# Layer 0's head by halves of the tokens, with another order of its first loads, in a two-layer float32 trunk on one core

## Chip, core and metric

One NeuronCore of a Trainium2 chip runs the kernel. The metric is the time of one execution in device microseconds. The engines are TensorE (PE; PEld is its weight load), VectorE (DVE), ScalarE (ACT), GpSimd (POOL) and SyncE (SP, which here issues most DMAs); 16 DMA engines move the data.

## The reference, cut to what matters

The model is one inference step of two layers over 640 tokens of width 1024: 128 prompt tokens, which take one condition vector, and 512 sample tokens, which take another.

```python
for i in range(2):
    sh, sc, gt = split(silu(cond) @ ada_w[i] + ada_b[i])   # adaLN, for both conditions
    h = rms_norm(y, norm_g[i]) * (1 + sc) + sh
    # layer 0: a, gate, z = split(h @ w_in + b_in); v = a * sigmoid(gate)
    #          v = depthwise_conv(v, 31 taps); v = silu(layer_norm(v))
    #          out = (v * silu(z)) @ w_out
    # layer 1: bidirectional state-space branch, chunked scan, gated norm, @ w_out
    y = y + gt * out
return rms_norm(y, final_norm_g)                           # and layer 1's final states
```

All is float32. A product with float32 accuracy is made of three matmuls in a reduced 32-bit format: each operand is split into a high part and the remainder, and high x high, high x low and low x high are added up in PSUM.

## The kernel before, in words

Channels lie on the 128 partitions: x is eight tiles (index k) of 128 channels by 640 tokens. The tokens are kept as two halves of 320, each with 64 prompt tokens ahead of 256 sample tokens. A tile product of layer 0 multiplies 128 output channels' weights with all eight k: per k and half three matmuls of 320 columns, so 48 in all. There are 48 tiles: a0 to a15, gates g0 to g15 (tile numbers 16 to 31) and z0 to z15.

The head of layer 0 is what the change is about; it runs in a scope of its own, with its own tiles. `loads` issues on SP first the constants, then x, k by k, and then for each of the eight adaLN blocks two pieces of 512 KB of w_ada (tile wa), with the weights of the first three tiles (u16, u0, u17; tile wf, 512 KB each) behind blocks 0, 1 and 2. `square0` squares x on ACT, `sums0` adds up the squares over the channels on PE into the tile rps, takes the root and the reciprocal for 640 tokens and spreads the result to all partitions (rs0). `ada_chain(k)` makes block k's scale and shift: eight small matmuls for each piece of w_ada into the tile ada, a copy of the row on ACT, a turn on PE (the matmul with ada_row), a bias on DVE (mod) and a scale on ACT (gsc). `modulation0(k)` then makes `modo = x * gsc * rs0` on DVE, h_hi (rounded, with the shift) on ACT and h_lo (the remainder) on DVE, each in one instruction for the prompt tokens of both halves and one for the sample tokens of both. `first_split` splits the weights of the first three tiles (high part wh on ACT, remainder wl on DVE or POOL), and `firsts` multiplies: for each k the three tiles u16 (in the trace u__99), u0 (u__100) and u17 (u__297), six matmuls each.

Behind the head `filler` runs the other 45 products in the order of PLAN0. A gate tile's sigmoid and its a tile give v; the depthwise convolution of tile i adds 31 taps on v: one is the start on ACT (cva), `NPOOL[i]` of them are made on ACT and added on POOL, the others are DVE instructions (line 808). The sums for the layer norm are made on PE behind products, as tiles become ready, the last two of them by `late_sums` (tile pst); `stats` spreads mean and inverse deviation (tile pmr), and then come normalising, gating and the output products.

The order on each engine is fixed when the program is built. Each step is a chain of operations with an assumed duration; a planner (`Order`) takes at each turn the operation that could begin first, by its model of the engines, and breaks ties by the table PRIO0. On the chip each engine works in that order and waits at an instruction whose inputs aren't there. DMAs from SP are issued in order, with at most eight on their way: the ninth waits for the landing of the first.

## Time and profile before

| | |
|---|---|
| Median of 3 runs (lowest to highest) | 1072.1 us (1069.98 to 1072.92) |
| Profiled execution, its own time | 1072.78 us |
| Its span, first to last instruction | 1071.0 us |
| Mean granted TensorE clock | 0.993 |
| PE busy / PEld | 1043.6 us (97%) / 973.2 us |
| DVE / ACT / POOL busy | 798.2 / 655.2 / 456.3 us |
| HBM read | 140.73 MB, 136 GB/s over the span |

Span times count from the first instruction; the execution's own time is 1.8 us longer. Busy shares are means over stages with different limits: PE's 97% says that it rarely stands still, not where. Where it does is read from windows and from the timeline, rows of which stand below.

### The profile page before, as it was taken

To read this page: it belongs to the slowest core of one execution; us is meant where nothing else is said; L and a number is where in the kernel's file an instruction comes from. 1 tells how busy PE (TensorE), PEld (TensorE's weight loads), DVE (VectorE), ACT (ScalarE), POOL (GpSimd) and SP (SyncE) were. 2 spreads that over 40 slices of the span, in tenths; PEclk is the share of its full clock that TensorE was granted. 3 is DMA by queue.
4 is the path that set the end of the run, shared out by engine and by line. 5 is a ranking of instruction groups with operands and counts; after the bars stand their busy time and mean duration, and the time that the engine had idled before them with its cause. 6 is when DMAs were issued, how large, how long until landed. Compare 5 with 4: busy or idle time off the path is not lost.

```text
span 1071.0 us, 19887 instructions
## 1 busy us (share of the span) xinstructions
PE 1043.6 (97%) x7892; PEld 973.2 (91%) x7892; DVE 798.2 (75%) x1191; ACT 655.2 (61%) x1081; POOL 456.3 (43%) x459
## 2 busy tenths in 40 slices
PE   5999999999999999999999999999999999999996
PEld 3899999999999999999999988998889988988886
DVE  2589999998997689103788787889767766985763
ACT  5468788787686588333576666685438553663542
POOL 0029989978596401110000155405532373445313
PEclk9999999999999999999999999999999999999998
DMA  9488888788766667675122644332633234343102
GB/s 358 193 248 205 195 218 197 177 212 209 175 142 135 144 133 157 151 170 114 59 75 73 142 102 128 93 95 71 147 83 96 89 99 129 108 101 107 41 21 99
DMA packets 86413, 146.94 MB, mean 137 GB/s; under 512 B 26800, under 2 KB 49712, under 8 KB 86320
## 3 DMA queue, kind: packets, MB, share of 16 engines
q1 hardware_dynamic: 77680, 114.73, 35.8%
...
q14 instruction: 31, 0.25, 0.1%
HBM read 140.73 MB, written 4.92 MB: 136 GB/s over the span
## 4 chain that ended last, share of the span: by engine, by line
PE 85%; DVE 7%; ACT 4%; DMA 2%; issue 1%; SPq 0%; POOL 0%; DVEq 0%; ACTq 0%
PE pz L1281 8%; PE o L1281 8%; PE xs L1281 4%; PE po L1563 3%; PE o L1819 3%; PE pst L1500 2%; DVE xs L1325 2%; PE C L1281 2%; PE B L1281 2%; PE py L1631 2%; PE o__4958 L156 1%; PE o__5267 L156 1%; PE o__5258 L156 1%; PE o__5245 L156 1%; PE o__5238 L156 1%; PE o__4948 L156 1%
## 5 line engine op out<-in xcount | busy, mean ns | idle before, releaser
L808 DVE SCALAR_TENSOR_TENSOR cva<-v,cst,cva 128x550 f32<-128x550 f32 (+12 forms) x346 | 270.1, 822 | 11.7 <-ACT cva L800 6.6
L880 POOL TENSOR_TENSOR cv<-cv,tp 128x490 f32<-128x490 f32 (+5 forms) x134 | 172.9, 1290 | 8.5
L839 ACT ACTIVATE tp<-v,cst 128x490 f32<-128x490 f32 (+5 forms) x134 | 92.4, 718 | 36.8 <-POOL cv L880 36.3
L423 ACT CAST wh<-wf 128x1024 fp32r<-128x1024 f32 x63 | 65.9, 1046 | 63.6 <-PE o__5267 L156 30.1
L1243 ACT CAST wh<-wf 128x1024 fp32r<-128x1024 f32 x53 | 55.5, 1046 | 66.5 <-PE pz L1281 24.4
L1281 PE MATMUL o<-yhl,wh 128*128 128x320 f32 x384 | 93.0, 329 | 0.0
L1281 PE MATMUL pz<-h_hi,wh 128*128 128x320 f32 x256 | 86.9, 339 | 0.0
L1569 POOL TENSOR_TENSOR y<-y,yo 128x512 f32<-128x512 f32 x32 | 47.2, 1474 | 75.9 <-DVE yo L1567 75.7
L1281 PE MATMUL pz<-h_hi,wl 128*128 128x320 f32 x256 | 79.1, 309 | 0.0
L1281 PE MATMUL pz<-h_lo,wh 128*128 128x320 f32 x256 | 79.0, 309 | 0.0
L1247 DVE TENSOR_TENSOR wl<-wf,wh 128x1024 fp32r<-128x1024 f32 x47 | 63.8, 1358 | 17.6 <-ACT wh L1243 17.5
L1281 PE MATMUL xs<-h_hi,wh 128*128 128x320 f32 x224 | 74.3, 332 | 0.8 <-ACT up L1312 0.8
L1281 PEld LDWEIGHTS o<-yhl,wh 128*128 128x128 f32 x384 | 64.0, 188 | 7.8 <-issue 7.8
L1281 PE MATMUL xs<-h_hi,wl 128*128 128x320 f32 x224 | 69.3, 309 | 0.1
L1281 PE MATMUL xs<-h_lo,wh 128*128 128x320 f32 x224 | 69.2, 309 | 0.0
L1325 DVE SCALAR_TENSOR_TENSOR xs<-up,cst,xs 128x642 f32<-128x642 f32 x64 | 62.6, 981 | 4.6 <-PE rms L1685 2.1
L433 ACT ACTIVATE wl<-wh 128x1024 fp32r<-128x1024 f32 x58 | 61.5, 1061 | 1.7
L1444 ACT ACTIVATE gf<-gf,cols 128x128 f32<-128x128 f32 x160 | 50.2, 390 | 18.0 <-DVE gf L1440 17.8
L434 POOL DMA_DIRECT2D wl<-w_in x43 | 37.5, 873 | 54.7 <-ACT wl L433 51.7
L1281 PE MATMUL o<-yhl,wl 128*128 128x320 f32 x192 | 59.4, 309 | 0.0
L1438 POOL TENSOR_TENSOR gb<-gb,cols 128x512 f32<-128x512 f32 x20 | 24.0, 1198 | 79.2 <-DVE xs L1325 65.1
L1281 PEld LDWEIGHTS pz<-h_hi,wh 128*128 128x128 f32 x256 | 48.3, 189 | 4.2 <-issue 4.2
...
## 6 DMA issues: line engine op xcount, KB each, us to landing
...
```

The source lines that it names most:

```text
L156: T.matmul(ps[:, b, at : at + t1 - t0], lhsT=w, rhs=h[:, t0:t1], start=first and n == 0, stop=last and n == 2)
L423: t = yield op(ACT, 1.05, lambda: S.copy(out=wh, in_=wf))
L433: yield op(ACT, 1.06, lambda: S.activation(out=wl, in_=wh.bitcast(F32), func=AF.Copy, scale=-1.0))
L808: t = yield op(VE, 0.24 + 0.01 * (hi - lo), lambda: V.scalar_tensor_tensor(out=rows64(accs[i], lo, hi), in0=rows64(vs[i], lo + d, hi + d), ...
L839: t = yield op(ACT, 0.72, lambda: S.activation(out=tp[:, :, 0 : hi - lo], in_=rows64(vs[i], lo + d, hi + d), func=AF.Copy, scale=w_dw(i, t ...
L880: t = yield op(PO, 1.3 + 0.019 * (hi - lo - 49), lambda: G.tensor_add(out=rows64(cv[i], lo, hi), in0=rows64(cv[i], lo, hi), in1=sgs["tp", ...
L1243: S.copy(out=cell["wh"], in_=cell["wf"])
L1247: e_.tensor_sub(out=cell["wl"], in0=cell["wf"], in1=cell["wh"].bitcast(F32))
L1281: T.matmul(ps[:, b, at_ : at_ + t1 - t0], lhsT=w_, rhs=t_[:, t0:t1], start=k == 0 and n == 0, stop=k == nk - 1 and n == 2)
L1325: t = yield op(VL, 0.89, lambda: V.scalar_tensor_tensor(out=acc, in0=u[:, d : d + PW], scalar=c("w_c", j * 5 + d), in1=acc, op0=ALU.mult, ...
L1444: t = yield op(ACT, 0.39, lambda: S.activation(out=gv[:, h_, :], in_=gv[:, h_, :], func=AF.Exp, bias=cols1[ch][:, o8 + h_ : o8 + h_ + 1]), ...
L1569: t = yield op(PO, 1.29, lambda: G.tensor_add(out=y, in0=y, in1=yo))
```

## The change

x is loaded as two halves of the tokens, each in four DMAs of two k; the squares of a half go to ACT or DVE, whichever the planner finds earlier; the sums, the root and the spread are made for each half apart, in a tile of the ring that held the adaLN rows. The third first tile, u17, gets its PSUM tile from the start (in the new program it is u__101). `modulation0` and `firsts` run for each half as chains of their own: half the columns in each instruction, twice as many instructions; the matmuls keep their 320 columns and their number, 144. The order of the first loads is now a list, LOADS0: x, block 0, the weights of u16 and u0, block 1, the weights of u17, then blocks 2 to 7. The tables PRIO0, PLAN0 and NPOOL have new values. One buffer of the ring st goes (11 to 10), and rs0 gets a tile of its own.

```diff
--- before.py
+++ after.py
@@ -38,11 +38,12 @@
 
 
...
-PLAN0 = "a1 z0 g2 a2 g3 a3 g4 a4 g5 a5 g6 a6 g7 a7 g8 a8 g9 a9 g10 z1 z2 a10 z3 g11 a11 g12 a12 g13 a13 g14 z4 a14 g15 z5 z6 a15 z7 z8 z9 z10 z11 z12 z13 z14 z15"
-NPOOL = (12, 6, 12, 6, 12, 11, 8, 10, 2, 8, 9, 8, 12, 4, 6, 8)
...
+PLAN0 = "a1 g2 a2 g3 a3 g4 a4 z0 g5 a5 g6 a6 g7 a7 g8 a8 g9 a9 g10 a10 g11 a11 g12 z1 z2 z3 a12 g13 a13 g14 a14 g15 a15 z4 z5 z6 z7 z8 z9 z10 z11 z12 z13 z14 z15"
+NPOOL = (9, 10, 12, 10, 3, 7, 11, 6, 12, 10, 12, 3, 9, 11, 3, 2)
+LOADS0 = (("x", 0), ("x", 1), ("a", 0), ("w", 0), ("w", 1), ("a", 1), ("w", 2), ("a", 2), ("a", 3), ("a", 4), ("a", 5), ("a", 6), ("a", 7))
 
 
@@ -437,7 +438,10 @@
 
 
         def stt(name):
-            return sp.tile([P, NT], F32, tag="st", bufs=11, name=name)
+            return sp.tile([P, NT], F32, tag="st", bufs=10, name=name)
+
+        def stt0(name):
+            return sp.tile([P, NT], F32, name=name)
 
         wa0, w0, x_sq, psx = {}, {}, {}, []
 
@@ -445,9 +449,12 @@
             def load(kb, fn, name):
                 t = yield op(DM, kb / 345.0, fn)
                 post(name, t + 2.2)
-            for k in range(KD):
-                yield from load(328, lambda: nc.sync.dma_start(out=x[k], in_=a["x"][:, k, :]), ("x", k))
-            for k in range(KD):
+            def load_x(b):
+                tok = slice(b * HN, b * HN + HN)
+                for k in range(0, KD, 2):
+                    yield from load(328, lambda: nc.sync.dma_start(out=xs_[:, k : k + 2, tok], in_=a["x"][:, k : k + 2, tok]), ("x", k, b))
+
+            def load_ada(k):
                 for q in range(2):
                     yield get("wa")
 
@@ -455,20 +462,24 @@
                         w = wa0[k, q] = sp.tile([P, 1024], F32, tag="wa", bufs=12, name="wa")
                         nc.sync.dma_start(out=w, in_=a["w_ada"][k, :, q * 1024 : q * 1024 + 1024])
                     yield from load(524, load_a, ("wa0", k, q))
-                if k < 3:
-                    if k < 2:
-                        yield get("wf")
-                        pool, bufs = gp, (2, 3, 3)
-                    else:
-                        pool, bufs = sp, (1, 1, 1)
-
-                    def load_w():
-                        w0["f", k] = pool.tile([P, 1024], F32, tag="wf", bufs=bufs[0], name="wf")
-                        nc.sync.dma_start(out=w0["f", k], in_=a["w_in1"][(16, 0, 17)[k]])
-                    yield from load(524, load_w, ("wf", k))
-                    start(first_split(k, pool, bufs), 0.0)
                 start(ada_chain(k), 0.0)
-                start(modulation0(k), 0.0)
+                for b in range(2):
+                    start(modulation0(k, b), 0.0)
+
+            def load_first(n):
+                if n < 2:
+                    yield get("wf")
+                    pool, bufs = gp, (2, 3, 3)
+                else:
+                    pool, bufs = sp, (1, 1, 1)
+
+                def load_w():
+                    w0["f", n] = pool.tile([P, 1024], F32, tag="wf", bufs=bufs[0], name="wf")
+                    nc.sync.dma_start(out=w0["f", n], in_=a["w_in1"][(16, 0, 17)[n]])
+                yield from load(524, load_w, ("wf", n))
+                start(first_split(n, pool, bufs), 0.0)
+            for what, n in LOADS0:
+                yield from {"x": load_x, "a": load_ada, "w": load_first}[what](n)
             yield from load(303, lambda: nc.sync.dma_start(out=cst0[0], in_=a["cst"][:, NCST : NCST + NCST0]), ("cst0",))
             run.clock[SP] = run.clock[DM] - 1.0
             start(weights(), run.clock[DM] - 1.0)
@@ -492,36 +503,40 @@
                 put("wf", t)
             post(("w0", n), t)
 
-        def square0():
-            yield get("px")
-            psx.append(px.tile([P, 2, 512], F32, tag="x", bufs=1, name="rps"))
-            rps = psx[0]
+        def square0(b):
+            yield get("adp")
+            ps = sps.tile([P, 512], F32, tag="ada", bufs=2, name="rps")
             for k in range(KD):
-                yield key(("x", k))
+                yield key(("x", k - k % 2, b))
                 yield get("st")
-
-                def square():
-                    x_sq[k] = stt("rms_sq")
-                    S.activation(out=x_sq[k], in_=x[k], func=AF.Square)
-                t = yield op(ACT, 0.73, square)
-                start(sums0(k, rps), t)
-
-        def sums0(k, rps):
-            t = yield op(PE, 0.4, lambda: quarter_sums(rps[:, 0, 320:480], x_sq[k], k == 0, k == KD - 1))
+                sq = stt("rms_sq")[:, 0:HN]
+                xv = x[k][:, b * HN : b * HN + HN]
+                t = yield either((ACT, 0.42, lambda: S.activation(out=sq, in_=xv, func=AF.Square)), (VL, 0.44, lambda: V.tensor_mul(out=sq, in0=xv, in1=xv)), bias=0.1)
+                start(sums0(k, b, ps, sq), t)
+
+        def sums0(k, b, ps, sq):
+            def add_up():
+                for q in range(2):
+                    r = 64 * b + 32 * q
+                    T.matmul(ps[r : r + 32, 0:QN], lhsT=ones[:, 0:32], rhs=sq[:, q * QN : q * QN + QN], start=k == 0, stop=k == KD - 1)
+            t = yield op(PE, 0.2, add_up)
             put("st", t)
             if k < KD - 1:
                 return
-            rq = sp.tile([P, QN], F32, name="rq0")
-            yield op(ACT, 0.42, lambda: S.activation(out=rq, in_=rps[:, 0, 320:480], func=AF.Sqrt, scale=1.0 / 1024, bias=epsb))
+            rows = slice(64 * b, 64 * b + 64)
+            rq = sp.tile([P, QN], F32, name=f"rq0{b}")[rows]
+            yield op(ACT, 0.42, lambda: S.activation(out=rq, in_=ps[rows, 0:QN], func=AF.Sqrt, scale=1.0 / 1024, bias=epsb[rows]))
             yield op(VE, 1.2, lambda: V.reciprocal(out=rq, in_=rq))
-            t = yield op(PE, 1.2, lambda: quarter_spread(rps, rq))
-            rs0.append(stt("rs0"))
-            t = yield op(ACT, 0.72, lambda: S.copy(out=halves(rs0[0]), in_=rps[:, :, 0:HN]))
-            put("px", t)
-            post(("rs0",), t)
-            yield op(ACT, 0.25, lambda: S.activation(out=junk, in_=rs0[0][:, 0:1], func=AF.Sigmoid), "sig")
-
-        rs0 = []
+
+            def spread_rq():
+                for q in range(2):
+                    T.matmul(ps[:, 160 + q * QN : 160 + q * QN + QN], lhsT=eye[rows, 64 * b + 32 * q : 64 * b + 32 * q + 1].broadcast_to([64, P]), rhs=rq, start=True, stop=True)
+            yield op(PE, 0.6, spread_rq)
+            t = yield op(ACT, 0.46, lambda: S.copy(out=rs0[:, b * HN : b * HN + HN], in_=ps[:, 160 : 160 + HN]))
+            put("adp", t)
+            post(("rs0", b), t)
+            if b:
+                yield op(ACT, 0.25, lambda: S.activation(out=junk, in_=rs0[:, 0:1], func=AF.Sigmoid), "sig")
 
         def ada_chain(k):
             yield get("adp")
@@ -545,47 +560,66 @@
             t = yield op(ACT, 0.39, lambda: ada_scale(0, k))
             post(("gs0", k), t)
 
-        def modulation0(k):
-            yield key(("gs0", k), ("rs0",), ("x", k))
+        def modulation0(k, b):
+            tok = slice(b * HN, b * HN + HN)
+            if not b:
+                h.append((hbuf("h_hi"), hbuf("h_lo")))
+            hi, lo = (z_[:, tok] for z_ in h[k])
+            yield key(("gs0", k), ("rs0", b), ("x", k - k % 2, b))
             yield get("st")
-            mo = stt("modo")
-            for cd, sl in SEGS:
-                t = yield op(VL, 0.34 + 0.4 * cd, lambda: V.scalar_tensor_tensor(out=halves(mo)[:, :, sl], in0=halves(x[k])[:, :, sl], scalar=gsc[0][:, k, cd : cd + 1], in1=halves(rs0[0])[:, :, sl], op0=ALU.mult, op1=ALU.mult))
-            hi, lo = hbuf("h_hi"), hbuf("h_lo")
-            h.append((hi, lo))
-            for cd, sl in SEGS:
-                yield op(ACT, 0.42 + 0.3 * cd, lambda: S.activation(out=halves(hi)[:, :, sl], in_=halves(mo)[:, :, sl], func=AF.Identity, bias=shift(0, k, cd)))
-            for cd, sl in SEGS:
-                t = yield op(VL, 0.34 + 0.4 * cd, lambda: V.scalar_tensor_tensor(out=halves(lo)[:, :, sl], in0=halves(mo)[:, :, sl], scalar=shift(0, k, cd), in1=halves(hi)[:, :, sl].bitcast(F32), op0=ALU.add, op1=ALU.subtract))
+            mo = stt("modo")[:, 0:HN]
+            xv, rv = x[k][:, tok], rs0[:, tok]
+            for cd, sl in SEGS[::-1]:
+                t = yield op(VL, 0.26 + 0.2 * cd, lambda: V.scalar_tensor_tensor(out=mo[:, sl], in0=xv[:, sl], scalar=gsc[0][:, k, cd : cd + 1], in1=rv[:, sl], op0=ALU.mult, op1=ALU.mult))
+            for cd, sl in SEGS[::-1]:
+                yield op(ACT, 0.3 + 0.16 * cd, lambda: S.activation(out=hi[:, sl], in_=mo[:, sl], func=AF.Identity, bias=shift(0, k, cd)))
+            for cd, sl in SEGS[::-1]:
+                t = yield op(VL, 0.26 + 0.2 * cd, lambda: V.scalar_tensor_tensor(out=lo[:, sl], in0=mo[:, sl], scalar=shift(0, k, cd), in1=hi[:, sl].bitcast(F32), op0=ALU.add, op1=ALU.subtract))
             put("st", t)
-            post(("h0", k), t)
-
-        def firsts():
+            post(("h0", k, b), t)
+
+        def firsts(b):
+            tok = slice(b * HN, b * HN + HN)
             for k in range(KD):
                 for n in range(3):
                     if not k:
                         yield key(("w0", n))
-                        if n == 2:
-                            yield get("px")
-                            first[2] = 17, px.tile([P, 2, 512], F32, tag="x", bufs=1, name="u17_")
-                    yield key(("h0", k))
-                    t = yield op(PE, 0.882, lambda: dense(first[n][1], w0["h", n], w0["l", n], k * 128, *h[k], k == 0, k == KD - 1))
+                    yield key(("h0", k, b))
+
+                    def step():
+                        hi, lo = h[k]
+                        ws, wls = w0["h", n][:, k * 128 : k * 128 + 128], w0["l", n][:, k * 128 : k * 128 + 128]
+                        for i, (w, t_) in enumerate(((ws, hi), (wls, hi), (ws, lo))):
+                            T.matmul(first[n][1][:, b, 0:HN], lhsT=w, rhs=t_[:, tok], start=k == 0 and i == 0, stop=k == KD - 1 and i == 2)
+                    t = yield op(PE, 0.441, step)
                     if k == KD - 1:
-                        post(("first", n), t)
-                        if n < 2:
-                            put("wh", t)
-                            put("wl", t)
+                        post(("first", n, b), t)
+                        start(first_done(n), 0.0) if b else None
+            post(("firsts", b), t)
+
+        def first_done(n):
+            t = yield key(("first", n, 0), ("first", n, 1))
+            if n < 2:
+                put("wh", t)
+                put("wl", t)
+            post(("first", n), t)
+
+        def all_firsts():
+            t = yield key(("firsts", 0), ("firsts", 1), *[("first", n) for n in range(3)])
             post(("firsts",), t)
 
-        first = [(16, mm("u16_")), (0, mm("u0_")), None]
-        for name, n in (("px", 1), ("st", 11), ("wa", 12), ("adp", 2)):
+        first = [(16, mm("u16_")), (0, mm("u0_")), (17, px.tile([P, 2, 512], F32, tag="x", bufs=1, name="u17_"))]
+        rs0 = stt0("rs0")
+        for name, n in (("st", 10), ("wa", 12), ("adp", 2)):
             run.ring(name, n)
         run.clock[:] = [6.0, 6.5, 2.0, 2.0, 2.0, 2.1]
         run.table = "sqrt"
         run.lead = 0.3
         start(loads(), 0.0)
-        start(square0(), 0.0)
-        start(firsts(), 0.0)
+        for b in range(2):
+            start(square0(b), 0.0)
+            start(firsts(b), 0.0, f"firsts{b}")
+        start(all_firsts(), 0.0)
         run.run(("firsts",))
         sp_ctx.close()
 
```

On SP, the loads from x on, before (x are eight DMAs; wa is w_ada, wf the first tiles' weights):

```order
L449 DMA x_67<-x 128x640 x8
L456 DMA wa_136<-w_ada 128x1024
L456 DMA wa_146<-w_ada 128x1024
L467 DMA wf_158<-w_in1 128x1024
L456 DMA wa_175<-w_ada 128x1024
L456 DMA wa_187<-w_ada 128x1024
L467 DMA wf_198<-w_in1 128x1024
L456 DMA wa_215<-w_ada 128x1024
L456 DMA wa_231<-w_ada 128x1024
L467 DMA wf_238<-w_in1 128x1024
L456 DMA wa_253<-w_ada 128x1024
```

and with the change:

```order
L455 DMA x_67<-x 128x2x320 x8
L463 DMA wa_150<-w_ada 128x1024
L463 DMA wa_167<-w_ada 128x1024
L478 DMA wf_184<-w_in1 128x1024
L478 DMA wf_202<-w_in1 128x1024
L463 DMA wa_214<-w_ada 128x1024
L463 DMA wa_223<-w_ada 128x1024
L478 DMA wf_236<-w_in1 128x1024
L463 DMA wa_250<-w_ada 128x1024
L463 DMA wa_266<-w_ada 128x1024
```

Block 1 (the second pair of wa) now stands behind two pieces of weights, and block 2 behind three.

On PE, from the spread of the norm to the first tile product, before (ada_160, ada_200 and ada_240 are blocks 0, 1 and 2):

```order
L209 MATMUL rps_101<-rq0_165,cst_60 128x160 x4
L131 MATMUL ada_160<-cst_60,ada_row_186 128x4
L537 MATMUL ada_200<-wa_175,scz_73 32x128 x8
L537 MATMUL ada_200<-wa_187,scz_73 32x128 x8
L537 MATMUL ada_240<-wa_215,scz_73 32x128 x8
L131 MATMUL ada_200<-cst_60,ada_row_230 128x4
L156 MATMUL u16__99<-h_hi_220,wh_195 128x320 x2
L156 MATMUL u16__99<-h_hi_220,wl_203 128x320 x2
L156 MATMUL u16__99<-h_lo_221,wh_195 128x320 x2
L537 MATMUL ada_240<-wa_231,scz_73 32x128 x8
```

and with the change (ada_187 and ada_227 are blocks 0 and 1; rps_104 is the norm of the second half):

```order
L533 MATMUL rps_104<-rq01_192,cst_60 128x160 x2
L132 MATMUL ada_187<-cst_60,ada_row_213 128x4
L552 MATMUL ada_227<-wa_214,scz_73 32x128 x8
L552 MATMUL ada_227<-wa_223,scz_73 32x128 x8
L132 MATMUL ada_227<-cst_60,ada_row_262 128x4
L593 MATMUL u16__99<-h_hi_169,wh_220 128x320
L593 MATMUL u16__99<-h_hi_169,wl_230 128x320
L593 MATMUL u16__99<-h_lo_170,wh_220 128x320
L593 MATMUL u0__100<-h_hi_169,wh_234 128x320
L593 MATMUL u0__100<-h_hi_169,wl_239 128x320
L593 MATMUL u0__100<-h_lo_170,wh_234 128x320
```

The first half block of block 2 stood ahead of the first product of u16 and now comes after it: twelve matmuls of k = 0, for u16 and u0 and both halves, stand ahead of it.

On DVE, around the end of convolution 14 (cv_3910 before, cv_3918 now; u__4182 and u__4002 are tile a15's products, ssum the sums' collection), before:

```order
L734 TENSOR_TENSOR ssum<-ssum,u__4089 128x320
L828 TENSOR_TENSOR cv_3910<-cv_3910,cva 128x640
L664 SCALAR_TENSOR_TENSOR v<-u__4182,cst_87,sg 128x640
L138 TENSOR_TENSOR mod_78<-u__4182,cst 128x4
L808 SCALAR_TENSOR_TENSOR cva<-v,cst_87,cva 128x10x53 x2
L808 SCALAR_TENSOR_TENSOR cva<-v,cst_87,cva 128x10x54 x2
```

and with the change:

```order
L768 TENSOR_TENSOR ssum<-ssum,u__4184 128x320
L842 SCALAR_TENSOR_TENSOR cva<-v,cst_87,cva 128x10x63
L842 SCALAR_TENSOR_TENSOR cva<-v,cst_87,cva 128x10x54
L842 SCALAR_TENSOR_TENSOR cva<-v,cst_87,cva 128x10x63
L842 SCALAR_TENSOR_TENSOR cva<-v,cst_87,cva 128x10x55
L862 TENSOR_TENSOR cv_3918<-cv_3918,cva 128x640
L842 SCALAR_TENSOR_TENSOR cva<-v,cst_87,cva 128x10x55
L842 SCALAR_TENSOR_TENSOR cva<-v,cst_87,cva 128x10x56 x2
L842 SCALAR_TENSOR_TENSOR cva<-v,cst_87,cva 128x10x57 x2
```

Before, v of tile 15 came only after the end of convolution 14, and all its taps on DVE behind it; now convolution 15 has begun earlier and its taps alternate with those of 14.

## Rows read from the trace of the kernel before

**Rows 1.** Windows: busy time (instructions) of PE, PEld, DVE, ACT, POOL; PEclk; DMA share; GB/s.

```profile
10.00:20.00 10.00, 6.42 (x106) 3.49 (x100) 4.10 (x7) 7.05 (x12) 0.00 (x0) 1.00 1.03 412
20.00:30.00 10.00, 7.58 (x86) 5.86 (x86) 5.56 (x11) 4.00 (x8) 0.00 (x0) 0.83 1.03 410
60.00:500.00 440.00, 439.99 (x3588) 432.64 (x3587) 346.10 (x477) 306.62 (x430) 261.65 (x291) 1.00 0.76 179
```

**Rows 2.** Waits of PE over the program: us in total, times, longest.

```profile
PE ada L537 <- DMA wa<-w_ada: 5.2, 4, 3.5
PE pt L1977 <- DVE t L1967: 2.0, 1, 2.0
```

**Rows 3.** Timeline of PE, head: start, us, instruction, [idle before <-releaser].

```profile
16.64 0.64 PE L537 MATMUL ada<-wa,scz 128*32 128x128 f32 x16 [0.51 <-DMA wa<-w_ada]
17.94 0.64 PE L537 MATMUL ada<-wa,scz 128*32 128x128 f32 x16 [0.65 <-DMA wa<-w_ada]
22.09 1.08 PE L537 MATMUL ada<-wa,scz 128*32 128x128 f32 x16 [3.51 <-DMA wa<-w_ada]
23.55 0.88 PE L156 MATMUL u__99<-h_hi,wh 128*128 128x320 f32 x2
...
54.39 0.46 PE L156 MATMUL u__297<-h_lo,wh 128*128 128x320 f32 x2
```

**Rows 4.** Timeline of ACT, head: row copy and first splits of weights.

```profile
14.80 0.27 ACT L541 COPY ada_row<-ada 128x128 f32<-128x128 f32 x1 [1.57 <-PE ada L537]
15.34 1.05 ACT L484 CAST wh<-wf 128x1024 fp32r<-128x1024 f32 x1 [0.28 <-DMA wf<-w_in]
...
20.70 1.04 ACT L484 CAST wh<-wf 128x1024 fp32r<-128x1024 f32 x1 [1.01 <-DMA wf<-w_in]
```

**Rows 5.** DMA queues in 9:10, 17:18, 31:32, 57:58, 1067:1068 us: packets, MB, share.

```profile
q1 hardware_dynamic: 170, 0.40, 104.4%
q8 instruction: 1, 0.02, 6.7%
q1 hardware_dynamic: 110, 0.41, 101.7%
q1 hardware_dynamic: 193, 0.35, 104.0%
q1 hardware_dynamic: 295, 0.36, 100.4%
```

**Rows 6.** Windows of one microsecond: granted clock (PEclk) in head and tail.

```profile
22.00:23.00 1.00, 0.91 (x16) 0.66 (x16) 1.00 (x1) 0.00 (x0) 0.00 (x0) 0.54 1.04 414
...
25.00:26.00 1.00, 1.00 (x18) 0.48 (x17) 0.36 (x1) 0.00 (x0) 0.00 (x0) 0.75 1.04 414
1041.00:1042.00 1.00, 0.42 (x4) 0.42 (x4) 0.46 (x1) 0.91 (x2) 0.00 (x0) 1.00 0.00 0
1042.00:1043.00 1.00, 1.00 (x8) 1.00 (x8) 0.18 (x1) 0.39 (x2) 0.00 (x0) 0.84 0.00 0
```

**Rows 7.** Groups by form on DVE, layer 0 (L559) and layer 1 (L1124): busy us, mean ns.

```profile
L559 DVE SCALAR_TENSOR_TENSOR h_lo<-modo,mod,h_hi 128x512 fp32r<-128x512 f32 x8 | 6.0, 748 | 1.0 <-ACT h_hi L557 1.0
L559 DVE SCALAR_TENSOR_TENSOR h_lo<-modo,mod,h_hi 128x128 fp32r<-128x128 f32 x8 | 2.8, 345 | 0.5 <-ACT h_hi L557 0.5
...
L1124 DVE SCALAR_TENSOR_TENSOR h_lo<-modo,mod,h_hi 128x256 fp32r<-128x256 f32 x16 | 7.7, 479 | 0.0
L1124 DVE SCALAR_TENSOR_TENSOR h_lo<-modo,mod,h_hi 128x64 fp32r<-128x64 f32 x16 | 4.5, 280 | 0.0
```

**Rows 8.** End of convolution 14: DVE's window and wait, ACT's square, PE's sums.

```profile
55.35:334.90 279.55, 268.58 (x370) 1.00 0.79 196
DVE cva L808 <- ACT cva L800: 4.9, 4, 2.0
334.94 0.74 ACT L708 ACTIVATE sq<-cv 128x640 f32<-128x640 f32 x1 [1.65 <-DVE cv L828]
L198 PE MATMUL pst<-cv,ones x16: 299/311/323, 336.8 to 365.8; 128*32 128x160 f32 x16
```

2 lines of the change are left out of this document (1 added, 1 removed).

## Prediction

> **What bounds the kernel now.** I read the windows first, then the waits of TensorE (PE), then the first 55 us engine by engine, then the stretch in which the convolution ends. The windows [rows 1] show where PE still has time to give: from 60 to 500 us it is busy 439.99 of 440 us, while it stands still 3.58 us in 10 to 20 and 2.42 us in 20 to 30. The waits [rows 2] name what it stands for there: the adaLN products wait 5.2 us for w_ada, 3.5 of them at one place; the next wait outside the head is 2.0 us, in layer 1. The timeline [rows 3] shows that place: half blocks of w_ada at 16.64 and 17.94, then nothing until 22.09, and the first tile product (u16, line 156) at 23.55. After that PE runs through; the last of the first three tiles' matmuls ends at 54.39 + 0.46 = 54.85, and the layer's other products follow at once. So whatever the head saves is worth its full amount at the end, if PE isn't made to wait later, and nothing else in layer 0 can give anything.
>
> What sets the head's pace is the DMA stream. The 512 KB pieces land 1.3 us apart: w16 at 15.34 [rows 4], the second block at 16.64 and 17.94 [rows 3]. Then one is late: w0 is there only at 20.70 [rows 4], 2.8 us after, and the third block's first half at 22.09. Between 17 and 18 us one instruction fetch takes 6.7% of 16 engines for a microsecond, 1.07 us of one engine [rows 5]; a piece is complete when its slowest engine is, so I take this for the cause, and it belongs to the time, not to the piece.
>
> **The change part by part.** *Order of the loads.* By the order on SP, the pieces behind x are block 0 (two), w16, w0, block 1 (two), w17, block 2; before, block 1 stood ahead of w0 and block 2's first half ahead of w17. On PE block 1 still stands whole ahead of the first tile product, and block 2's first half no longer does. What PE must have for u16 is thus the sixth piece behind x where it was the seventh. The sixth is at 20.70, if the late step stays where it is. From the start of the half block at 22.09 to the first product at 23.55 are 1.46 us at half clock [rows 3, 6], so 0.73 at the full one; the ACT copy of the row, 0.27 [rows 4], now lies in between, with 0.1 for handing over. First product: 20.7 + 0.73 + 0.27 + 0.1 = 21.8.
>
> *Work behind it.* The number of PE instructions is the same, 144 matmuls of 320 columns for the three tiles in both. From 23.55 to 54.85 are 31.3 us. Of these PE spent about 1.95 at half clock: the granted clock falls a little after 22 and is back in the middle of 25 to 26 [rows 6]; that is 0.97 lost. Block 2's first half comes on top, 0.64 less its overlap, 0.57 [rows 3]. At the full clock: 31.3 - 0.97 + 0.57 = 30.9, so the three tiles end at 52.7, 2.15 earlier.
>
> *Halves on DVE and ACT.* Each block's scaling and its low part were two instructions of 128x512 and two of 128x128 (0.748 + 0.345 for a pair) and are now four of 128x256 and four of 128x64 (0.479 + 0.280) [rows 7]: 2 x 1.09 = 2.19 us become 4 x 0.76 = 3.04 us, 0.85 more per block, 6.8 over eight. ACT's high parts grow alike. DVE was busy 5.56 of the 10 us from 20 to 30 [rows 1], so 0.85 in each 3.8 us of PE's work per block fits, and the first half is ready before the second. I take nothing for it; without that cover it would be at most 0.85 for the first block, since later blocks are a block ahead.
>
> *Squares and the norm by halves.* They begin earlier, and four squares go to DVE, which was idle. This ends nothing: the scaling needs block 0, which lands behind the last of x anyway. Worth nothing, either way.
>
> *x in pieces of 320 tokens.* Each row of a DMA was 2560 B and is now two of 1280 B, so each of the 16 engines moves 128 packets for x in place of 64. 2560 B took 104.4% of 16 engine-microseconds over 170 packets, 98 ns; 2048 B took 86 ns (104.0%, 193); 4096 B 148 ns (101.7%, 110) [rows 5]. A load of 1280 B isn't in the trace. Stores of exactly this shape took 54.5 ns (100.4%, 295): two are 109, 11 more than 98, times 64 is 0.7 us. From 2048 and 2560 B a straight line gives 68 ns for 1280: two are 136, 38 more, 2.4 us. Below nothing I exclude: two packets for one can't be cheaper by any of these rows. I take 1.2, nearer the row of the same shape. The stream is full (398 GB/s at 9 to 10, 406 at 31 to 32), so all that lands behind x comes later by it. The rows thus show that a packet has a fixed part: 2.0 KB moved at 354 GB/s, 4 KB at 406 [rows 5].
> The Trainium skill (DMA: Bandwidth & Descriptors, "Why small descriptors are slow (HBM only)") gives a fixed cost of some 3 cycles to each packet beside one cycle per 32 bytes. By it 1280 B cost 43 cycles and 2560 B 83, so x would take 3.6% longer, an estimate of 0.24 us, and this change would come out about 1 us faster than my sum. The trace shows a larger fixed part than that.
>
> *Plan, priorities, taps.* The tables also order the rest of layer 0 anew: z0 goes from second to eighth product, a15 comes ahead of z5 and z6, and 130 taps go over GpSimd in place of 134. From the mean and variance spreads to the end of the program PE's order is the same, and so is its count before it: 45 products, 16 adaLN blocks, 16 sums. So nothing is gained there; what could be lost is the rival below.
>
> **Sum.** 2.15 - 1.2 = 0.95 us. The profiled execution took 1072.78, 1.78 beside its span of 1071.0; it would be 1071.8. It stands 0.7 above the median of the three, 1072.1, so the forecast for a median is 1071.2.
>
> **Rivals.**
> *The clock falls again.* For: between the second half of block 1 and its forerunner PE does next to nothing for 2.1 us, and from the end of block 0's work to the first product it has, by the sum above, little more than two half blocks of 0.64 to do. The clock fell after 3.51 us of standing still, but in the tail also after a mere 0.7, when one-column products had gone before: busy 0.42 in 1041 to 1042, and 0.84 granted in the next [rows 6]. Against: the gaps of 0.5 and 0.65 before 17.94 left it at the full clock [rows 3], and the longest gap is now 2.1. If it falls, the products start at 1.2 GHz, 2.4 GHz being the full one: 3.4 us at half clock cost 1.7, in place of the 0.97 of before and the 0.73 ahead of the first product (in both sums), so 1.4 more than I have: 1072.6.
> *The sixth piece isn't late.* If the fetch comes after it, block 1 is there at 17.94 + 1.3 = 19.3, and the first product waits for its own halves instead, which I put at 21 (w0's low part and the scaling behind it): 0.8 to 1.4 more gained, 1069.9.
> *DVE is late with the convolution (the slower side).* The square of convolution 14 ended at 334.94 + 0.74 = 335.7 and its sums on PE began at 336.8 [rows 8], 1.1 later. In the new order ten more DVE instructions stand ahead of that end, nine of them taps, at 268.58/370 = 0.73 us each: 7.3 us. PE has only 18 more matmuls ahead of the sums, 2.6 us. DVE must thus give up 7.3 - 2.6 - 1.1 = 3.6 of its 11 idle microseconds there (279.55 less 268.58). Waits for others make up much of that, 4.9 for ACT's first write of an accumulator [rows 8]; the earlier a tiles make room for this. If none of it went, PE would stand 3.6 us at the sums, in order, and everything behind it too: 1071.2 + 3.6 = 1074.8. It decides from the point where less than 3.6 is given up.
>
> **How the numbers follow.** Forecast 1071.2: 0.42. Clock falls, 1072.6: 0.27. Sixth piece early, 1069.9: 0.14. DVE late, 1072 to 1075: 0.12. Anything else, 0.05. The cost of x's packets alone moves the forecast from 1070.7 to 1072.4; the three runs of before lie 2.9 apart, so a median of few runs is uncertain by about 1. The range is 1068.8 to 1074.6. What can be told from no change is 0.3%, 3.2 us: faster means below 1068.9, for which the early piece, packets at the price of the stores and a full clock must come together (2.15 + 1.4 - 0.7 = 2.85) and the runs' spread must help, 0.10. Slower means above 1075.3: DVE late and the clock down, 0.06. The rest, 0.84, is no difference.
>
> **What would show it.** Right: the first u16 product near 21.8 + 1.2 = 23.0, only half a microsecond earlier than now, because x's packets give back most of the lead; the last of the three tiles' matmuls ending near 53.9; x's packets at 60 to 70 ns; no PE wait between 60 and 500. Wrong: the first product at 21 or at 24, a granted clock of 0.5 behind it, or a wait of PE for the sums near 335, each of which is one of the rivals.

## The result and the profile after

The changed kernel takes 1075.36 us (median of 14 executions, 1074.36 to 1079.94) where the kernel before takes 1070.82 (14 executions beside it): a ratio of 1.0042, 95% interval 1.0029 to 1.0056. It is slower by 4.5 us; the forecast was 0.9 faster, and the range ended 0.8 below the measured time. The forecast of 1071.2 set out from 1072.1, a median of three; the fourteen executions put the kernel before at 1070.82.

The profiled execution of the changed kernel is the longest of its fourteen: 1079.94 us, span 1078.2. A second profile, of the same kernel run again beside the experiments, has a span of 1074.2 and its own time of 1075.97; it stands beside the first throughout, since what the two disagree on turns out to be half of the story.

First the windows of the changed kernel, to hold against [rows 1]:

```profile
10.00:20.00 10.00, 9.15 (x80) 6.00 (x74) 2.29 (x2) 4.99 (x12) 0.00 (x0) 1.00 1.05 410
20.00:30.00 10.00, 6.21 (x65) 5.16 (x65) 8.70 (x21) 7.25 (x17) 0.00 (x0) 0.66 1.01 405
60.00:500.00 440.00, 438.34 (x3572) 431.40 (x3571) 347.12 (x482) 304.91 (x428) 257.12 (x288) 1.00 0.75 180
```

Two things are new. From 10 to 20 us PE is busy 9.15 us where it was 6.42, with fewer instructions (80, not 106); from 20 to 30 the granted clock is 0.66 where it was 0.83, and DVE is busy 8.70 us where it was 5.56, beside a DMA stream that is as full as before. And from 60 to 500 PE stands still 1.66 us where it never did. The waits of PE, against [rows 2], name both places:

```profile
PE ada L132 <- ACT ada_row L556: 3.5, 1, 3.5
...
PE u__3266 L678 <- DVE ssum L768: 1.0, 1, 1.0
...
PE u__3590 L132 <- ACT ada_row L669: 0.7, 1, 0.7
```

No wait for w_ada is left in this execution. The timeline of PE in the head, against [rows 3]:

```profile
20.47 1.08 PE L552 MATMUL ada<-wa,scz 128*32 128x128 f32 x32 [0.26 <-DVE mod L139]
25.09 0.59 PE L132 MATMUL ada<-cst,ada_row 128*128 128x4 f32 x2 [3.54 <-ACT ada_row L556]
25.54 0.61 PE L593 MATMUL u__99<-h_hi,wh 128*128 128x320 f32 x1
...
57.75 0.31 PE L593 MATMUL u__101<-h_lo,wh 128*128 128x320 f32 x1
```

The first product is at 25.54 (before 23.55), the three tiles end at 58.06 (before 54.85). The same timeline of the second profile of the changed kernel:

```profile
20.96 1.08 PE L552 MATMUL ada<-wa,scz 128*32 128x128 f32 x16 [1.98 <-DMA wa<-w_ada]
22.43 0.59 PE L132 MATMUL ada<-cst,ada_row 128*128 128x4 f32 x2 [0.39 <-ACT ada_row L556]
22.88 0.61 PE L593 MATMUL u__99<-h_hi,wh 128*128 128x320 f32 x1
...
54.68 0.31 PE L593 MATMUL u__101<-h_lo,wh 128*128 128x320 f32 x1
```

Here the first product is at 22.88, where the forecast had 23.0, and the tiles end at 54.99. Instructions and their order are the same in both. What differs is how long PE took for the same small matmuls before. Groups of PE by form (busy us, mean ns): first the changed kernel, the first execution, at 11 to 13 and at 17 to 19 us:

```profile
L521 PE MATMUL rps<-rms_sq,ones 128*32 128x160 f32 x12 | 1.8, 474 | 0.8 <-ACT rms_sq L514 0.8
...
L552 PE MATMUL ada<-wa,scz 128*32 128x128 f32 x26 | 1.9, 419 | 0.0
```

and the kernel before, at 12.4 to 13 us and, for the measure, at 22 to 23, where its granted clock reads 0.54 [rows 6]:

```profile
L198 PE MATMUL rps<-rms_sq,ones 128*32 128x160 f32 x8 | 0.5, 311 | 0.2 <-ACT rms_sq L505 0.2
...
L537 PE MATMUL ada<-wa,scz 128*32 128x128 f32 x16 | 1.1, 419 | 3.5 <-DMA wa<-w_ada 3.5
```

419 ns is what an adaLN product takes at 1.2 GHz (278 at 2.4), 473 what a sum takes (299 to 311). So PE begins at half clock, though the clock's column reads 1.00 there. In the kernel before the sums had come down to 311 by 12.4 us; in the changed kernel's first execution the adaLN products still took 419 at 18.6. The Trainium skill (TensorE: Matmul & The Clock Gate, "What's actually happening") says that the throttled state is the default and that activity releases it; these rows agree, and show a release that comes some 7 us later in one execution than in another. It isn't the halves alone: in the other traces of this head without fillers at the start the sums came down between 10 and 13 us, and in one of plan alone, whose head is the old one, the half clock lasted to between 14 and 15.

What the late release did is read on ACT. The timeline of ACT in the first execution:

```profile
20.45 0.39 ACT L148 ACTIVATE gsc<-mod,cst 128x2 f32<-128x2 f32 x1 [0.41 <-DVE mod L139]
...
21.05 1.04 ACT L495 CAST wh<-wf 128x1024 fp32r<-128x1024 f32 x1
22.12 1.28 ACT L539 ACT_TABLE_LOAD   x1
...
23.52 1.37 ACT L575 ACTIVATE h_hi<-modo,mod 128x256 fp32r<-128x256 f32 x4
24.80 0.24 ACT L556 COPY ada_row<-ada 128x128 f32<-128x128 f32 x1
```

Block 0's scale came at 20.45 (before 16.88), and behind it a split of weights, a table load and four high parts stand ahead of block 1's row, for which PE waits. In the second execution the same scale is at 17.80 and the row at 22.14.

Where the 7.2 us of the first pair of profiles and the 3.2 of the second went (spans 1078.2 and 1074.2, before 1071.0), cut at the end of the three tiles and at layer 1's first turn (pt, at 590.1 before):

| | first execution | second |
|---|---|---|
| head, to the end of the three tiles (58.06, 54.99; before 54.85) | +3.2 | +0.1 |
| from there to the turn (537.1, 537.6; before 535.2) | +1.8 | +2.4 |
| from the turn to the end (483.1, 481.6; before 480.9) | +2.2 | +0.7 |

The middle term is the two waits, 1.0 to 1.1 and 0.7. The last term is the clock again: in both executions it fell behind PE's stand of 2.06 us at the turn, and in the first the tail lost 3.3 us at half clock (busy time by what the clock lacks, added up over windows of one microsecond) where before lost 1.7. (By this count the two executions lost 3.3 and 1.7 us more than before, which is more than the 2.2 and 0.7 that they took longer here; the clock is the largest part of the term, not an exact account of it.) Windows of the second execution, just there:

```profile
592.00:593.00 1.00, 0.40 (x4) 0.40 (x4) 1.00 (x4) 1.00 (x1) 0.00 (x0) 0.93 0.00 0
593.00:594.00 1.00, 1.00 (x6) 0.96 (x5) 0.96 (x3) 0.96 (x3) 0.00 (x0) 0.50 0.83 90
594.00:595.00 1.00, 1.00 (x6) 1.00 (x5) 0.96 (x2) 0.22 (x1) 0.00 (x0) 0.50 1.00 381
```

The kernel before stands there as long (2.0 [rows 2]) and kept its clock.

### The profile page after: what moved, and what is told of

Read it like the earlier page. It is cut to its first block, busy times and chain, and to the rows that moved or that the text cites. A ratio compares the mean times of both kernels' runs of the same rounds, so it can differ in the third digit from the quotient of the medians.

```text
span 1078.2 us, 19933 instructions
## 1 busy us (share of the span) xinstructions
PE 1051.9 (98%) x7892; PEld 982.0 (91%) x7892; DVE 802.8 (74%) x1232; ACT 653.2 (61%) x1097; POOL 451.2 (42%) x455
## 4 chain that ended last, share of the span: by engine, by line
PE 86%; DVE 6%; ACT 5%; POOL 1%; issue 1%; DMA 0%; SPq 0%; DVEq 0%; POOLq 0%; ACTq 0%
PE pz L1315 8%; PE o L1315 8%; PE xs L1315 5%; PE C L1315 3%; PE po L1597 3%; PE o L1853 3%; PE pst L1534 2%; PE B L1315 2%; PE py L1665 2%; DVE xs L1359 1%; PE o__5064 L157 1%; PE o__5327 L157 1%; PE o__5314 L157 1%; PE o__5336 L157 1%; PE o__5307 L157 1%; PE o__5054 L157 1%
## 5 line engine op out<-in xcount | busy, mean ns | idle before, releaser
L842 DVE SCALAR_TENSOR_TENSOR cva<-v,cst,cva 128x560 f32<-128x560 f32 (+13 forms) x350 | 270.3, 821 | 8.8 <-ACT cva L834 4.7
L914 POOL TENSOR_TENSOR cv<-cv,tp 128x490 f32<-128x490 f32 (+5 forms) x130 | 165.7, 1275 | 8.5
L873 ACT ACTIVATE tp<-v,cst 128x490 f32<-128x490 f32 (+5 forms) x130 | 90.0, 718 | 30.5 <-POOL cv L914 29.7
L1277 ACT CAST wh<-wf 128x1024 fp32r<-128x1024 f32 x53 | 55.5, 1046 | 67.1 <-PE pz L1315 24.2
L1281 DVE TENSOR_TENSOR wl<-wf,wh 128x1024 fp32r<-128x1024 f32 x47 | 63.1, 1342 | 19.6 <-ACT wh L1277 19.5
```

The lines of the kernel that those rows point to most:

```text
L842: t = yield op(VE, 0.24 + 0.01 * (hi - lo), lambda: V.scalar_tensor_tensor(out=rows64(accs[i], lo, hi), in0=rows64(vs[i], lo + d, hi + d), ...
L873: t = yield op(ACT, 0.72, lambda: S.activation(out=tp[:, :, 0 : hi - lo], in_=rows64(vs[i], lo + d, hi + d), func=AF.Copy, scale=w_dw(i, t ...
L914: t = yield op(PO, 1.3 + 0.019 * (hi - lo - 49), lambda: G.tensor_add(out=rows64(cv[i], lo, hi), in0=rows64(cv[i], lo, hi), in1=sgs["tp", ...
L1277: S.copy(out=cell["wh"], in_=cell["wf"])
L1281: e_.tensor_sub(out=cell["wl"], in0=cell["wf"], in1=cell["wh"].bitcast(F32))
```

## The experiments

Ratios are to runs of the kernel before on the same chip (23 to 31 executions, median 1072.5 to 1072.7), with 95% intervals; 0.001 is 1.07 us. They differ from the ratios of the medians by up to 0.0006. "Product" is u16's first, "tiles" the end of the three tiles, in the profiled execution.

| kernel | ratio | interval | product | tiles |
|---|---|---|---|---|
| changed, again | 1.0041 | 1.0029 to 1.0054 | 22.9 | 55.0 |
| head alone | 1.0008 | 0.9997 to 1.0019 | 22.9 | 54.8 |
| head alone, again | 1.0007 | 0.9997 to 1.0017 | 22.3 | 55.3 |
| plan alone | 1.0013 | 1.0003 to 1.0023 | 23.4 | 56.0 |
| plan alone, again | 1.0017 | 1.0007 to 1.0027 | 22.8 | 55.5 |
| changed, PE busy from the start | 1.0012 | 1.0004 to 1.0021 | 22.0 | 54.8 |
| changed, 26 matmuls in the gap | 1.0032 | 1.0020 to 1.0044 | 27.9 | 58.5 |
| changed, old order of loads | 1.0029 | 1.0016 to 1.0041 | 21.4 | 55.9 |
| changed, turn filled | 1.0034 | 1.0024 to 1.0045 | 22.9 | 54.9 |
| before, head filled | 0.9998 | 0.9989 to 1.0007 | 22.7 | 53.2 |
| head alone, head filled | 0.9985 | 0.9977 to 0.9994 | 21.9 | 52.5 |
| the same, turn filled too | 0.9983 | 0.9974 to 0.9993 | 22.0 | 52.6 |
| changed, head and turn filled | 1.0013 | 1.0002 to 1.0025 | 22.2 | 52.8 |
| the same, old NPOOL | 0.9992 | 0.9981 to 1.0002 | 21.6 | 52.2 |

**Head alone, plan alone.** The old PLAN0, NPOOL and priorities behind the head in the changed kernel, and the new ones in the kernel before:

```
-PLAN0, NPOOL, PRIO0 (but for the head's names) of one kernel
+those of the other
```

> The changed kernel with the old PLAN0, NPOOL and the old priorities behind the head: only the head by halves is left of the change. Theory: the slowdown is two terms, the head (+3.2 us: in the changed kernel the last matmul of the three tiles ends at 58.06 where it was 54.85) and two waits of PE between 250 and 290 us that the new plan brings (0.98 and 0.7). Then this kernel keeps the head's loss alone: ratio to before 1.003 (+3.2 us), and no PE wait of over 0.3 between 60 and 500. Rival: the waits come from the late head and not from the plan, and stay: ratio 1.0045. The PE order of the head is the same as in the changed kernel, so first product near 25.5 in both theories.

> The kernel before with the new PLAN0, NPOOL and the new priorities behind the head; its head is untouched. Theory of two terms: the three tiles still end near 54.85, the two waits between 250 and 290 (0.98 and 0.7 us) are there, ratio to before 1.0016 (+1.7 us). Rival: the waits are a consequence of the late head; then none here, ratio 1.000.

The plan's term is as expected: 1.0013, with waits of 0.8 and 0.7 us and 537.0 us from the tiles to the turn, in a program whose head is the old one; and head alone has neither wait (535.2). So the waits come from the tables. The head's term was expected at 3.2 and came out at 0.8, with an interval that holds no change at all: its execution here had the product at 22.9. The 25.54 of the first profile was one execution's late clock, not the head's price. The trace of plan alone shows something of the old head, too: its three tiles end at 56.0 (55.5 when it was run again), later than the 54.85 of the one trace from which the forecast was read, and it lost 3.2 us at half clock in the head in both where that trace lost 1.7.

**The changed kernel again, and both parts again.**

> The changed kernel once more, unaltered, on the same chip as the runs beside it. Head alone came out at 1.0008 and plan alone at 1.0013, together 1.0021, where the whole change measured 1.0042 on another chip. If the two terms add up and nothing else is in it, this run gives 1.0015 to 1.0030 here; if the change has a third term that neither part shows, 1.004 again. The clock theory adds: its head has the same order as that of head alone, whose sums came down to the full clock near 13 us and whose first product stood at 22.8; so the profile here shows a first product anywhere between 22 and 25.5, the earlier the sooner the sums drop from 472 to 311 ns.

> Head alone (the changed head, the old plan) once more, unaltered, beside plan alone and the changed kernel on one chip. First time 1.0008 (0.9997 to 1.0019). If the parts add up to the whole, the middle of both runs is nearer 1.002; if there is a third term, it stays at 1.001 or below.

> Plan alone (the old head, the new tables behind it) once more, unaltered. First time 1.0013 (1.0003 to 1.0023). From the trace its two waits and what stands around them are 1.7 us between the end of the three tiles and layer 1's first turn, 537.3 us against 535.6: 1.0016. It stays there if the waits are all of it.

1.0041 again; head 1.0007, plan 1.0017. The parts together are 2.4 us (0.8 and 1.6 over both runs each), the whole 4.4. A third term of about 2 us, with an uncertainty of about 1.5, is not in either part.

**PE busy from the start.**

```
+        for _ in range(12):
+            T.matmul(first[0][1][:, 0, 0:128], lhsT=ones, rhs=ones, start=True, stop=True)
         run.run(("firsts",))
```

> The changed kernel with twelve matmuls of 128x128 ones ahead of everything else on PE, into the tile of u16, which is begun anew later. They fill PE from 1 to 6 us, when it stands still otherwise. Theory of the clock: in the changed head the sums of squares run at 472 ns each up to 16.5 and the adaLN products at 420 up to 18.6 us, the half clock, where before they came down to 311 and 279 near 12 us; PE was thereby what ended the norm of the second half and block 0's adaLN row 4 us late. With PE warm the sums take 300 ns, the second half's sums end near 14.3 and not 16.9, the first u16 product comes at 22 to 23 and not at 25.5, and the three tiles end near 54 to 55: 3 to 4 us less than the changed kernel, ratio to before 1.000 to 1.0015. Rival 1, the vector and scalar engines: the two low parts of weights (1.22 us each), the table load of 1.28 and eight small steps between block 0's scale and the first product set the time; then the first product moves by less than 1 us. Rival 2, x in 1280 B packets: no change at all.

2.9 thousandths less than the changed kernel, 3.1 us, as the theory had it. The head of the second profile doesn't account for that: its tiles ended at 55.0, and here they end at 54.8. The groups on PE from 7 to 20 us:

```profile
L521 PE MATMUL rps<-rms_sq,ones 128*32 128x160 f32 x60 | 5.4, 305 | 1.0 <-ACT rms_sq L514 1.0
L552 PE MATMUL ada<-wa,scz 128*32 128x128 f32 x52 | 2.5, 279 | 2.9 <-DMA wa<-w_ada 2.9
```

All sums are at the full clock, PE waits for DMA again, and the first product is at 22.0. The clock then fell all the same, at 20.2 us, behind 17 to 20 where PE was busy 0.73 of 3 us, and 3.0 us were lost at half clock; so the tiles ended no earlier than 54.8.

**26 matmuls in the gap.**

```
+            if k == 1:
+                26 matmuls of 128x320 into u17's tile, operands the high part of u16's weights
             row = ap.tile([P, P], F32, tag="ada_row", bufs=2, name="ada_row")
```

> The changed kernel with 26 matmuls of 128x320 on PE behind block 1's adaLN products (operands: the high part of u16's weights; into u17's tile, which is begun anew later). They fill the 3.5 us in which PE stands still before the first product, at 21.6 to 25.1. Theory: the first product stays near 25.5, but the granted clock does not fall from 23 to 29.6, where about 4 us of products ran at half clock; the three tiles end 1.7 to 2 us earlier, near 56.2, ratio to before 1.002 to 1.0025. Rival: the products of the first blocks are paced by the halves' modulation on DVE, so that a faster PE only waits; then the three tiles end at 57.5 or later.

Wrong as a test: here the clock had fallen at 19.5 already, ahead of the fillers, and they ran at half speed, 26 from 21.9 to 27.6, in front of the first product (27.9). The gap that I sized them for was the first profile's. It shows only that a filler behind the fall runs at half clock itself. Its ratio rests on five executions.

**Old order of the loads.** `LOADS0` as before: block 0, w16, block 1, w0, block 2, w17.

> The changed kernel with the loads in the order of before: block 0, the weights of u16, block 1, the weights of u0, block 2, the weights of u17. On PE u0's products stand behind u16's of both halves; the twelve rows ahead of u16 are the same. The forecast's own reason said that the new order of the loads brings the lead of 2 us: then this kernel is about 1 to 2 us slower than the changed one. Theory now: the first product waits for ACT and DVE behind block 0's scale and for block 1's row, and block 1 now lands 1.3 us earlier, so it is the same or up to 1 us faster.

The first product came 1.5 us earlier (21.4), as the theory of block 1's row has it and against the forecast's reason, but the tiles ended 0.9 later, at 55.9, with u0's products pushed back. 1.0029 against 1.0041 isn't told apart by these intervals.

**The head filled, in the new and in the old head.**

```
                 def products():
+                    idle({(1, 0): 6, (1, 1): 4}.get((k, q), 0))
...
+            if k == 1:
+                idle(3)
```

with the twelve at the start; `idle(n)` is n matmuls of 128x128 ones into u16's tile. In the old head: `{(1, 1): 2, (2, 0): 12}`.

> The head by halves with the old plan, with twelve matmuls of 128x128 ones at the start of PE, and 6, 4 and 3 more where PE waits for block 1 (ahead of its first and second piece and behind them). All go into u16's tile, which is begun anew later. Clock theory: PE is at the full clock from 6 us to the end of the head; first product 21.5 to 22, no half clock behind it (3.0 us lost there in the kernel with the twelve alone, whose three tiles end at 54.8), so the three tiles end near 52 and the time is 2.5 to 3 us below head alone (1.0008): ratio to before 0.998. Rival: modulation by halves on the vector engine, 3.04 us a block and the splits besides, cannot feed a PE at the full clock, so PE waits between the blocks: three tiles end at 54 or later, ratio 1.000.

> The kernel before with the same twelve matmuls at the start, and 2 and 12 more ahead of block 1's second piece and block 2's first, where PE stood still for 3.51 us. Clock theory: no half clock from 22 to 25.5 (0.97 us of work lost behind the first product, 0.7 ahead of it): first product near 23, three tiles end near 53.4 where they ended at 54.85, ratio 0.9985 to 0.999. If the head by halves is worth anything by itself, the filled head by halves lies below this by the 1 to 1.5 us by which its needed piece lands earlier; if not, both are alike. Rival: the clock is no matter of how much PE does, and falls all the same: ratio 1.000.

The head by halves: 0.9985, product at 21.9, no half clock, tiles at 52.5. The rival (modulation can't feed PE at the full clock) is out. The old head: tiles at 53.2. In its one trace the clock fell at 11.5 us, between the sums, and at the turn, and over its twelve executions the mean granted clock is 0.9927, near the 0.9921 of the kernel before beside it, where the filled halves have 0.9944. So its fillers raised the clock little, and 0.9998 is no clean measure of what a held clock gives the old head. In the two traces both ran at the full clock from the first product on, and there the halves end 0.7 us earlier; that the halves by themselves are worth this is not shown beyond these two. PE of the head by halves (with the turn filled too), where [rows 3] had 3.51 us of standing still:

```profile
18.69 0.65 PE L557 MATMUL ada<-wa,scz 128*32 128x128 f32 x16 [0.42 <-DMA wa<-w_ada]
19.26 1.16 PE L543 MATMUL u__99<-ones 128*128 128x128 f32 x8
20.48 0.64 PE L557 MATMUL ada<-wa,scz 128*32 128x128 f32 x16
21.06 0.94 PE L543 MATMUL u__99<-ones 128*128 128x128 f32 x6
21.83 0.28 PE L132 MATMUL ada<-cst,ada_row 128*128 128x4 f32 x2
21.97 0.39 PE L600 MATMUL u__99<-h_hi,wh 128*128 128x320 f32 x1
```

**The turn filled.** Eight matmuls of 128x128 ones ahead of the turn at which PE waits 2.06 us, in the changed kernel and in the filled head with the old plan:

```
             def turn():
+                for _ in range(8 if n == 2 else 0):
+                    T.matmul(pt[:, 384:512], lhsT=ones, rhs=ones, start=True, stop=True)
```

> The changed kernel with eight matmuls of 128x128 ones ahead of the turn in layer 1 at which PE waits 2.06 us for DVE (near 590 us). In both traces of the changed kernel the granted clock fell behind that wait, to a half for 3.5 us (1.66 us lost, about 0.9 of it seen at the end); in the trace of before, of head alone and of plan alone it did not. Theory: that fall is the third term beside head and plan; kept away here, the ratio to before is 1.003 where the changed kernel had 1.0041. Rival: it falls as often in the kernel before, and the third term is elsewhere: 1.004 again.

> The head by halves with the old plan and the filled head (0.9985), and the same eight matmuls at layer 1's turn as in the run beside it. Theory: 0.9980, with no half clock anywhere but in the last 40 us. Rival: 0.9985, as without them, since the clock mostly holds there when the head was filled (it held in the one trace).

1.0034 lies between the two theories, and its interval holds both. The clock held at the turn, as meant; but in the tail it lost 3.4 us here, where before lost 1.7 [rows 6], with the same instructions in the same order. 0.9983 is the fastest kernel of this study, 1.8 us below the kernel before (1.3 by the medians) and no better than 0.9985 within what can be told. Its windows, against [rows 1]:

```profile
10.00:20.00 10.00, 8.65 (x108) 6.11 (x109) 5.33 (x7) 8.05 (x16) 0.00 (x0) 1.00 1.04 406
20.00:30.00 10.00, 9.94 (x140) 8.07 (x139) 7.77 (x24) 5.93 (x18) 0.00 (x0) 1.00 1.03 408
60.00:500.00 440.00, 439.99 (x3588) 432.76 (x3587) 344.09 (x475) 306.59 (x427) 259.24 (x289) 1.00 0.73 177
```

**The whole change, filled; and with the old NPOOL.**

> The whole change with the filled head and the filled turn of layer 1: it differs from the version measured at 0.9983 in the tables behind the head alone. Theory: the 1.8 us that the whole change lost beyond its two parts are falls of the clock, which the fillers keep away; then only the plan's 1.6 us stand between the two, ratio to before 0.9983 + 0.0015 = 0.9998, and the trace shows the two waits (0.8 to 1.1 and 0.7) and 1.7 us more between the three tiles and the turn. Rival: head and new plan hinder one another by something else; then the ratio is 1.0015 or more and the trace shows a third wait.

> The same with the old NPOOL: how many taps of each convolution are made on GpSimd is as before, the order of the products and the priorities are new. The first wait is one for DVE, which stands in twelve taps in a row ahead of the sums' collection; the second is one for ACT's copy of a row behind a table load. If the split of the taps makes them, both go or change and the ratio falls by up to 1.6 us to 0.9983; if the order of the products does, they stay at 0.8 and 0.7 and the ratio is that of the run beside it.

With head and clock alike, the new tables cost 1.0013 against 0.9983, 3.2 us and not 1.6. The trace has no third wait: 1.0 and 0.7, 537.1 us from the tiles to the turn against 535.2. In the two traces the rest stands in the tail, where the clock fell here (3.2 us lost) and not in the other. But that is one execution of each: over the twelve of each the mean granted clocks are 0.9941 and 0.9944, some 0.4 us apart, so the tail's clock does not explain the medians, and the other 1.6 us are not located. With the old NPOOL the second wait is gone, the first stays at 0.8, 536.2 to the turn, and the time falls to 0.9992: under the new order the split of the taps makes ACT's wait, and DVE's is there with either split, so it comes with the order of products or the priorities. The 2.2 us by which the time falls are more than the 0.9 that the trace shows up to the turn.

What the two waits are, in the second profile of the changed kernel. DVE, ahead of the collection of the sums in the tile that PE needs next, ACT, which reads the same tile (sz is the gate made of it), and PE behind them:

```profile
233.11 20.01 DVE L842 SCALAR_TENSOR_TENSOR cva<-v,cst,cva 128x590 f32<-128x590 f32 x25
253.16 0.49 DVE L768 TENSOR_TENSOR ssum<-ssum,u__3054 128x320 f32<-128x320 f32 x1
...
251.03 1.28 ACT L714 ACT_TABLE_LOAD   x1
252.33 0.79 ACT L714 ACTIVATE sz<-u__3054,cst 128x640 f32<-128x640 f32 x1
...
253.70 1.08 PE L678 MATMUL u__3266<-wa,scz 128*32 128x128 f32 x32 [1.15 <-DVE ssum L768]
```

and ACT, ahead of the row that PE turns, and PE behind it:

```profile
283.84 1.28 ACT L685 ACT_TABLE_LOAD   x1
285.14 0.79 ACT L685 ACTIVATE sg<-u__3484,cst 128x640 f32<-128x640 f32 x1
285.83 0.26 ACT L669 COPY ada_row<-u__3484 128x128 f32<-128x128 f32 x1
...
286.14 0.39 PE L132 MATMUL u__3590<-cst,ada_row 128*128 128x4 f32 x2 [0.71 <-ACT ada_row L669]
```

Twenty-five taps in a row, not the twelve of the expectation above, hold the DVE queue for 20.0 us while the sums wait to be collected (the kernel before had at most twelve in a row in the same 20 us); a table load and a sigmoid hold ACT's. That the taps alone make the first wait is not shown. In all ten traces with the new order the collection began 0.02 to 0.04 us behind the end of sz on ACT, and with the old NPOOL, where the taps ended sooner, DVE stood idle 0.25 us for sz. By that trace, where PE still waited 0.8 us, fewer taps ahead of the collection leave most of this wait to ACT.

**What stays open.** Of the 4.4 us, 1.6 are the plan's waits (measured twice, both waits seen in every trace with all the new tables) and 0.8 the head with the clock as it falls (measured twice, each time with an interval that holds 1). About 2 are not settled. The traces show where such time can go. In the tail, whose order is the same in all, the half clock cost 3.3 and 1.7 us in the changed kernel, and with the new tables otherwise 1.7 to 1.8 (three traces), 3.2, 3.4, 4.3 and twice nothing; with the old tables 1.7 in three traces and nothing in three. At the turn it fell in five of the twelve traces without a filler there, with either.

One trace a kernel can't tell how often that happens, but the span and the mean granted clock of every execution are on record. Span times what the clock lacks of full is, on the mean, 8.0 to 8.8 us in the kernel before, 8.5 and 8.7 in plan alone, 9.7 and 10.0 in head alone, 9.9 and 10.0 in the changed kernel, with standard errors of 0.3 to 0.5 (1.1 for the six of the second run of the changed kernel). This counts stretches in which PE stands still as well. So far as it shows, the new tables do not make the falls likelier; the head by halves loses some 1.3 us more than the old head; and the whole loses no more than head alone. The 2 us are thus not more of the falls that the granted clock shows. What it can't show is the half clock ahead of the release, where it reads 1.00. The twelve matmuls at the start, which do away with that, took 3.1 us off the changed kernel with this measure unchanged at 9.9, which points there; but head alone has the same start without the 2 us, and with the head filled the new tables still cost 1.6 us more than their waits. So the third term stays open.

## Why the prediction was wrong

Two steps failed: the three tiles at the full clock, and the tables that could lose nothing but at one place. The forecast was 0.95 us less and the changed kernel takes 4.4 more; of these 5.4 the head is some 1.75, the tables 1.6, and about 2 have no cause that a run shows.

- *The needed piece and the first product.* 23.0 forecast; 22.9, 22.9, 22.9, 22.3 in four traces of this head, 25.5 in one. The size was right, in part by luck: x's packets cost some 0.2 to 0.5 and not 1.2, and in their place PE was at half clock ahead of the product, and behind block 1's second piece (19.6 to 21.0 when its products begin, 20.7 forecast) it waits 0.4 to 1.4 us more for ACT's copy of the row, which I had put at 0.27. Four high parts and a table load stand ahead of it on ACT; the order showed that, and I hadn't looked at ACT.
- *x's packets.* The step "I take 1.2" was too large. In 9 to 10 us of the first execution:

```profile
q1 hardware_dynamic: 319, 0.39, 105.9%
```

53 ns a packet; two are 106 where one of 2560 B took 98 [rows 5], 0.5 us over x. By bytes landed from 1 to 20 us (6.72 MB on the mean of twelve traces of this head, 6.56 to 6.82; 6.82 of four of the old one, 6.80 to 6.84) 0.1 MB is missing, 0.24 us at 410 GB/s. The traces of this head spread over more than that, so the bytes say little but that the cost is small. The row of the stores (54.5 ns) was the right neighbour, the straight line through larger packets was not. The estimate by the Trainium skill's rule (DMA: Bandwidth & Descriptors, "Why small descriptors are slow (HBM only)") was 0.24: the bytes agree with it, the packets' time is twice that.
- *"At the full clock: 31.3 - 0.97 + 0.57 = 30.9".* This step failed. PE fell to half clock at 17 to 23 us in every trace of this head without fillers and came back at 25 to 29.9, so that tiles ended at 54.8 to 58.1 and not at 53.9: from the first product to their end 31.9 to 33.0 us in the five with the new order of loads, where the step had 30.9. It was the first rival (clock falls again, 1.4 more, 0.27), and its price is near: 0.95 forecast gain less 1.4 is +0.45, measured +0.8 with an uncertainty as large. (The 1.4 doesn't come out of the rival's own terms: 0.97 and 0.73 are 1.7, which would give +0.75.) With the clock held, the head alone gives what the step said: 30.6 us from the first product on, and the end at 52.5 and 52.6, forecast 52.7 without x's packets. The trace that the step set out from was also the old head's best of three: 31.3 us there, 32.6 in both of plan alone. The row that the rival rested on, a fall in the tail behind little work and not behind none, should have made it the likeliest case: the sum itself left PE little more than two half blocks of 0.64 to do ahead of 21.8.
- *The clock before the first product* was taken as full because its column read 1.00. The durations, 473 and 311 ns for the same matmul, stood in the same trace.
- *"So nothing is gained there; what could be lost is the rival below".* This step failed too. The tables cost 1.6 us with the old head, and 3.2 with the filled one, which my rivals had at a chance of 0.12 and at the wrong place: I had looked at the end of convolution 14, where PE did not wait. PE waits 80 and 50 us earlier, at a tile's sums and at a turn. PE had 439.99 busy of 440, so any instruction that PE needs and that moved behind a long run on DVE or ACT was a candidate; I checked one.
- *Rivals.* DVE late with convolution 14: no wait there in any trace. The sixth piece early: with PE at the full clock up to it the product is at 21.6 to 22.2. ACT copies block 1's row at 21.0 to 21.4 there, behind a table load and the high parts of the first half; that rival had 21, set by the halves' own steps.
